# Spreading the RMS reciprocals over the partitions: one fp32 diagonal in four 128-column products, or two fp32r diagonals in two 512-column products

## The chip, the cores and the metric

One core of one Trainium2 chip runs the whole kernel. The metric is the device time of one execution in microseconds (us). Engines are named as the profile names them: PE is TensorE (PEld its weight load), DVE is VectorE, ACT is ScalarE, POOL is GpSimd, SP is the queue that issues most DMAs.

## What is computed

One layer of a hybrid decoder trunk over 1024 tokens of width 1024, in float32. Two RMS norms, one before the input projection and one behind the output projection, are what the change is about:

```python
def rms_norm(x, g):
    xf = x.astype(jnp.float32)
    y = xf * lax.rsqrt(jnp.mean(xf * xf, axis=-1, keepdims=True) + NORM_EPS)
    return (y * g.astype(jnp.float32)).astype(x.dtype)

h = rms_norm(x, g_pre[i])
proj = h @ w_in[i]            # six slices: S5, LRU and merge-gate inputs
...                           # S5 branch -> z_s, RG-LRU branch -> z_l
merged = jax.nn.sigmoid(gate_s) * z_s + jax.nn.sigmoid(gate_l) * z_l
x = x + rms_norm(merged @ w_out[i], g_post[i])
x = x + (p[i] @ w_ple[i]) * jax.nn.sigmoid(x @ w_ple_gate[i])
```

## The kernel before

Everything is kept transposed: channels lie on the 128 partitions, tokens on the free axis, in two halves of 512 tokens (`HT`). A float32 product is made of three products of fp32r parts (`three`, lines L316 and L318): each operand is split into a high part, which ACT writes by a copy into an fp32r tile, and a low part, which DVE (or a DMA with an accumulate, lines L225 and L226) forms as value minus high part. Weights come in blocks of 128x128, four to a "quad" `wq`; the class `Weights` loads them into four raw buffers, splits them (L222 on ACT, L234 on DVE) and keeps six quads in a ring, so that they are made some quads ahead of their use.

PE, DVE, ACT and POOL are in a manual schedule: each runs its instructions in the order in which the code writes them. Work that is to run beside the products of PE is written as generators; `tick()` takes one step of each between quads.

The statistics of a norm are made by `tok_rstd`, a generator in three steps. First PE sums the squares over the partitions, so that the sums of 128 tokens stand in one column of a PSUM tile `pst` (L388). Then DVE and ACT compute, on 8 columns (4 for a half), the variance, the square root (L393, ACT), its reciprocal and one Newton step (L394 to L398), and DVE multiplies the identity by each column, which gives one 128x128 diagonal for 128 tokens (L401). In the third step a matrix of ones times each diagonal (L406) puts the reciprocal of every token on all partitions, in a PSUM tile `psb` for each half.

It is called three times.

- **pre**, at the start of the kernel, for all 1024 tokens. At that time PE computes the eight rows `ps_ple` of `p @ w_ple` (m = 0 to 7, 12 products each), in PSUM tiles of 1024 columns of which there are three (`pw2`); row m = 7 uses the tile of row m = 4. ACT copies each row to SBUF (`evict`, L743). The second step of `tok_rstd` stands in the code behind the products of m = 5 and ahead of the evictions of m = 4 and m = 5; the third stands in the middle of the products of m = 7. Behind it `h_hi` (L727 on DVE, L728 on ACT) and `h_lo` (L733) normalise x and split it, for the first products of the input projection (`ps_u`).
- **post1**, for the second half of the tokens, beside the last products of the output projection (`oV`). Its results feed a chain of steps on DVE and ACT (`post_half`), one for each of the eight channel blocks: mix times `psb` (L1562), times the gain plus the residual (L1563), the high part on ACT (L1364), the low part on DVE (L1371). The first products of the gate (`ps_pg`) follow it.
- **post0**, for the first half, beside the products of the gate for the second half. On ACT a sigmoid of a finished gate row (L1589) stands right behind its square root, with the load of the table for it; on DVE the product and the sum with that row (L1590, L1591) stand ahead of the chain of post0.

Of the kernel before, what the change touches and what calls it, by code (L numbers as in the profile page):

```python
# [9 lines left out]
F32 = mybir.dt.float32  # L10
F32R = mybir.dt.float32r
I32 = mybir.dt.int32
AF = mybir.ActivationFunctionType
ALU = mybir.AluOpType
# [3 lines left out]
P = 128  # L18
NT = 1024
HT = 512  # L20
ND = 8
# [114 lines left out]
class Weights:  # L136
# [99 lines left out]
    def next(self):  # L236
        self.make(self.pos)
        self.lows(self.pos)
        t = self.done[self.pos]
        n = QUADS[self.pos][3]  # L240
        self.pos += 1
        return [(t[:, 0, b, :], t[:, 1, b, :]) for b in range(n)]
# [10 lines left out]
def tile_hybrid_trunk(  # L253
# [11 lines left out]
    V, S, G, T = nc.vector, nc.scalar, nc.gpsimd, nc.tensor  # L265
# [10 lines left out]
    def page(i, name, dt=F32R):  # L276
        return page_pool[i].tile([P, 2 * NT], dt, tag=f"pg{i}", name=name)
# [10 lines left out]
    def cst(shape, name, value=None, dt=F32):  # L288
        t = const.tile(shape, dt, name=name)
        if value is not None:  # L290
            V.memset(t, value)
        return t

    ones = cst([P, P], "ones", 1.0)
    ident = cst([P, P], "ident")
    make_identity(nc, ident)
    halfpi = cst([P, 1], "halfpi", math.pi / 2)
    cp_t = cst([P, sum(n for _, n in CPAR)], "cp_t")
    sp8 = cst([P, NL], "sp8")
    nsp8 = cst([P, NL], "nsp8")  # L300
    cp = {}
    o = 0
    for nm, n in CPAR:
# [19 lines left out]
    def bank(name):  # L323
        return pp.tile([P, HT], F32, tag="pp", name=name)
# [58 lines left out]
    def tok_rstd(v, ssqs, n, name, res, diag):  # L383
        nch = n // P
        ps = px.tile([P, HT], F32, tag="px", name=f"pst_{name}")
        for c in range(nch):
            for j, ssq in enumerate(ssqs):
                T.matmul(ps[:, c:c + 1], ssq[:, c * P:(c + 1) * P], ones[:, 0:1], start=j == 0, stop=j == len(ssqs) - 1)  # L388
        yield
        v = v.rearrange("p (i n) -> p i n", i=4)  # L390
        var, r, t, sd = (v[:, i, :nch] for i in range(4))
        V.tensor_scalar(var, ps[:, :nch], 1.0 / (ND * P), EPS, ALU.mult, ALU.add)
        S.activation(sd, var, AF.Sqrt)  # L393
        V.reciprocal(r, sd)  # L394
        V.tensor_tensor(t, r, r, ALU.mult)
        V.tensor_tensor(t, t, var, ALU.mult)
        V.tensor_scalar(t, t, -0.5, 1.5, ALU.mult, ALU.add)
        V.tensor_tensor(r, r, t, ALU.mult)  # L398
        diag = diag.rearrange("p (c t) -> p c t", c=nch)
        for c in range(nch):  # L400
            V.tensor_scalar(diag[:, c, :], ident, r[:, c:c + 1], None, ALU.mult)  # L401
        yield
        for h in range(n // HT):
            pb = px.tile([P, HT], F32, tag="px", name=f"psb_{name}_{h}")
            for c in range(4):
                T.matmul(pb[:, c * P:(c + 1) * P], ones, diag[:, 4 * h + c, :], start=True, stop=True)  # L406
            res.append(pb)
        yield

# [40 lines left out]
    def quarter(t):  # L450
        return t.rearrange("p (k n) -> p k n", n=HT)
# [7 lines left out]
    pro = pctx.enter_context(tc.tile_pool(name="pro", bufs=1))  # L459
    x_half = [pool.tile([P, 4, NT], F32, name=f"xt{i}") for i, pool in enumerate((pro, prob))]  # L460

    def xt(k, s=slice(0, NT)):
        return x_half[k // 4][:, k % 4, s]

    def two_rows(i, name, dt=F32):
        return page(i, name, dt).rearrange("p (k n) -> p k n", k=2)

    sdp = two_rows(9, "sdp")
    ssq = sdp[:, 0]
# [4 lines left out]
    NPAR = sum(n for _, n in SPAR)  # L474
    NPT = NPAR - 2048
    pt = scratch[:, :NPT]
    braw = page(7, "braw", F32)

    ET = mybir.EngineType
    ctx.enter_context(tc.manual_schedule(engines={ET.PE, ET.DVE, ET.Activation, ET.Pool}))  # L480
# [221 lines left out]
    def square(k):  # L702
        sq = sqs[k % 2][:, k // 2 % 2] if k else ssq
        if k in (1, 3):
            (V if k == 1 else G).tensor_tensor(sq, xt(k), xt(k), ALU.mult)
        else:
            S.activation(sq, xt(k), AF.Square)
        if k:
            adds.append(sq)
# [4 lines left out]

    rb = []
    ssqs = [ssq]
    stats = tok_rstd(pro.tile([P, 4 * ND], F32, name="rs_pre"), ssqs, NT, "pre", rb, sdp[:, 1])
    hq = {}

    def hplain(k, h):  # L720
        hi, lo = hq[f"B{1 + k // 4}{1 + h}"]
        return hi[:, k % 4, :], lo[:, k % 4, :]

    def h_hi(k):
        for h in range(2):
            xs = xt(k, HALF[h])
            V.scalar_tensor_tensor(xs, xs, gpre[:, k:k + 1], rb[h], ALU.mult, ALU.mult)  # L727
            S.activation(hplain(k, h)[0], xs, AF.Copy)  # L728
# [12 lines left out]
    def evict(m):  # L741
        sb = ple_sb[m // 2][:, m % 2]
        S.activation(sb, rows_ps[m], AF.Copy)  # L743
        nc.sync.dma_start(ple_d[m], sb)
# [34 lines left out]
    h_lo(0)  # L779
    evict(7)  # L780
    h_hi(1)
    nc.sync.dma_start(braw[:, :1024], spar[:, NPT:NPT + 1024])
    S.activation(d_skip, pt[:16, NPT - 32:], AF.Copy)

# [448 lines left out]
    def ysr(j):  # L1233
        return ysf[j // 2][:, j % 2]
# [28 lines left out]
    for j in range(NS):  # L1263
        t, y = et[:, j % 2], ysr(j)
# [22 lines left out]
    PG = (9, 18, 11, 2, 3, 16, 17, 4, 5, 12, 13, 10, 14, 15, 0, 1, 6, 7, 8)  # L1287
# [19 lines left out]
    for p_ in range(4):  # L1307
# [9 lines left out]
        z, w_, v = (bank(f"b{n}{p_}") for n in "ZWV")  # L1317
# [28 lines left out]
    def quads8(idx, name):  # L1346
        t = [[quarter(page(idx[2 * s + q], f"{name}{s}{q}")) for q in range(2)] for s in range(2)]
        return lambda s, k: t[s][k // 4][:, k % 4, :]
# [3 lines left out]
    def mgrow(d):  # L1352
        return mgt[d // 2][:, d % 2]
# [9 lines left out]
    def lagged(lo, src, hi):  # L1363
        S.activation(hi, src, AF.Copy)  # L1364
        late.append((lo, src, hi))
        flush(1)

    def flush(n=0):
        while len(late) > n:
            lo, src, hi = late.pop(0)  # L1370
            V.tensor_tensor(lo, src, hi.bitcast(F32), ALU.subtract)  # L1371
# [41 lines left out]
    for n, d in enumerate(F_ROWS):  # L1413
        if n:
            sgs_load()
        for h, ps in enumerate(brows(ysr_, f"F{d}", NS)):
            r = mgrow(d)[:, HALF[h]]
# [15 lines left out]
    def x1(k, h):  # L1433
        return x1p[k // 2][:, k % 2, HALF[h]]
# [20 lines left out]
    def last_op():  # L1455
# [12 lines left out]
    sq, ssq = ([t[:, HALF[i]] for i in range(2)] for t in (  # L1468
        h2.tile([P, NT], F32, tag=f"g{j}", name=n) for j, n in enumerate(("sq", "ssq"))))
    counts, pending = [0, 0], [[], []]  # L1470

    def mixt(row, h):
        if mix[h][row // 4] is None:
            mix[h][row // 4] = quarter(page(PG[((0, 2), (18, 11))[h][row // 4]], f"mix{h}{row // 4}", F32))
        return mix[h][row // 4][:, row % 4, :]
# [11 lines left out]
    def add_square(h):  # L1487
        for t in pending[h]:
            V.tensor_tensor(ssq[h], ssq[h], t, ALU.add)
        pending[h].clear()  # L1490
# [53 lines left out]
    def post_half(h):  # L1544
        out_ = []
        while squares[h]:
            square(h, squares[h].pop(0))
            yield
        add_square(h)
        st = tok_rstd(dg[:, 2, 32 * h:32 * h + 32], [ssq[h]], HT, f"post{h}", out_, dg[:, h, :])  # L1550
        if h == 0:
            yield
        next(st)
        next(st)
        yield
        for _ in st:
            pass
        rb = out_[0]
        x1hl[h] = hl = quads8(mpg[h], f"x1hl{h}")
        for k in range(ND):  # L1560
            mk = mixt(k, h)
            V.tensor_tensor(mk, mk, rb, ALU.mult)  # L1562
            V.scalar_tensor_tensor(x1(k, h), mk, gpost[:, k:k + 1], x1(k, h), ALU.mult, ALU.add)  # L1563
            lagged(hl(1, k), x1(k, h), hl(0, k))
            if k == ND - 1:
                flush()
            yield
# [44 lines left out]
                    V.tensor_tensor(sb[:, q], sb[:, q], x1(m, h)[:, q], ALU.add)  # L1612
                nc.sync.dma_start(out[m * P:(m + 1) * P, h * HT + cs.start:h * HT + cs.stop], sb[:, cs])

    dg = quarter(page(PG[1], "diags", F32))
    bg.append(post_half(1))
    for name, row in (("T4", 1), ("T4", 3), ("T4", 5), ("T4", 7), ("B21", 4), ("B21", 6)):
        c, ps = mixt(row, 0), bank(f"oV{row}")
# [3 lines left out]
    plp, sbp = (quarter(page(PG[i], n, F32)) for i, n in ((9, "plp"), (10, "sbp")))  # L1622
    drain()
    bg.append(post_half(0))
    gate_half(1, x1hl[1])
    drain()
# [68 lines left out]
```

## Time and profile before

| | |
|---|---|
| median of 3 runs | 932.66 us (932.24 to 932.68) |
| the profiled execution | 932.37 us, of which the span of its instructions is 930.6 us |
| PE busy | 923.1 us of the span (99%), 4228 matmuls |
| DVE busy | 625.0 us (67%) |
| ACT busy | 469.6 us (50%) |
| POOL busy | 150.3 us (16%) |
| granted TensorE clock, mean | 0.999 |

A timeline row reads: start and duration in us, engine, line, operation, output and inputs, form, count of merged instructions, and in square brackets the idle time of the engine before it with what ended it. Successive matmuls overlap in the records, so the distance between starts is what a matmul costs in a stream, not its duration. The same holds for successive ACT instructions, whose starts lie a little closer than their durations.

### The profile page before, as it was taken

What the parts mean: (1) busy time and instruction counts of PE and PEld (TensorE: products, weight loads), DVE (VectorE), ACT (ScalarE), POOL (GpSimd) and SP (SyncE); (2) the same over time, 40 slices, a digit from 0 to 9 for tenths busy, and PEclk for the clock granted to TensorE, in tenths of its full rate; (3) what the DMA queues carried; (4) which work ended last, traced back from release to release, by engine and by line L of the source; (5) the groups of instructions that cost most, each with busy time, mean ns of one, the idle gap of its engine ahead of it and who ended that gap; (6) DMA issues with size and microseconds to landing.
All of it is one profiled execution on the core that took longest, in us unless ns stands there. A gap on an engine that the chain in (4) does not pass through costs nothing.

```text
span 930.6 us, 11716 instructions
## 1 busy us (share of the span) xinstructions
PE 923.1 (99%) x4228; PEld 759.7 (82%) x4228; DVE 625.0 (67%) x977; ACT 469.6 (50%) x714; POOL 150.3 (16%) x159
## 2 busy tenths in 40 slices
PE   9999999999999999999999999999999999999997
PEld 7888888888888888888888888888888887887876
DVE  6985566666664446776666667687862798886863
ACT  6643233444443257666666668444434355558531
POOL 1318012212220000000000000022322126422100
PEclk9999999999999999999999999999999999999999
DMA  9745456554623211111111117811479965499951
GB/s 356 277 126 158 126 141 168 173 166 138 178 90 107 74 29 52 51 51 45 52 51 51 52 44 208 296 41 57 141 261 238 271 164 203 122 244 231 301 181 52
DMA packets 70442, 134.21 MB, mean 144 GB/s; under 512 B 18416, under 2 KB 32880, under 8 KB 70384
## 3 DMA queue, kind: packets, MB, share of 16 engines
q1 hardware_dynamic: 64768, 122.72, 41.5%
q0 software_dynamic: 5472, 10.49, 6.5%
q8 instruction: 33, 0.54, 0.2%
q10 hardware_dynamic: 144, 0.26, 0.1%
q14 instruction: 25, 0.20, 0.1%
HBM read 95.30 MB, written 27.53 MB: 132 GB/s over the span
## 4 chain that ended last, share of the span: by engine, by line
PE 96%; DVE 2%; issue 0%; DMA 0%; ACT 0%
PE ps_L L318 16%; PE ps_L L316 8%; PE ps_rg L318 8%; PE ps_rx L318 8%; PE ps_pg L318 6%; PE ps_rx L316 4%; PE ps_rg L316 4%; PE ps_F L318 3%; PE ps_u L318 3%; PE bZ L318 3%; PE ps_pg L316 3%; PE pg L318 2%; PE bW L318 2%; PE bX L318 2%; PE ps_ple L318 2%; PE ps_ea L318 2%
## 5 line engine op out<-in xcount | busy, mean ns | idle before, releaser
L318 PE MATMUL ps_L<-hB,wq 128*128 128x512 f32 x640 | 197.4, 390 | 0.0
L318 PEld LDWEIGHTS ps_L<-hB,wq 128*128 128x128 f32 x640 | 120.2, 188 | 24.5
L316 PE MATMUL ps_L<-hB,wq 128*128 128x512 f32 x320 | 127.0, 397 | 0.0
L222 ACT ACTIVATE wq<-wraw 128x512 fp32r<-128x512 f32 (+1 forms) x188 | 112.5, 614 | 24.3 <-issue 9.4
L234 DVE TENSOR_TENSOR wq<-wraw,wq 128x512 fp32r<-128x512 f32 (+1 forms) x152 | 104.0, 700 | 3.2 <-ACT wq L222 3.2
L318 PE MATMUL ps_rg<-hB,wq 128*128 128x512 f32 x320 | 98.7, 390 | 0.0
L318 PE MATMUL ps_rx<-hB,wq 128*128 128x512 f32 x320 | 98.7, 390 | 0.0
L318 PE MATMUL ps_pg<-x1hl,wq 128*128 128x512 f32 x240 | 75.2, 394 | 0.5 <-DVE x1hl L1371 0.5
L316 PEld LDWEIGHTS ps_L<-hB,wq 128*128 128x128 f32 x320 | 60.1, 188 | 13.4 <-issue 1.7
L318 PEld LDWEIGHTS ps_rg<-hB,wq 128*128 128x128 f32 x320 | 60.1, 188 | 12.9
L318 PEld LDWEIGHTS ps_rx<-hB,wq 128*128 128x128 f32 x320 | 60.1, 188 | 12.9
L1075 DVE SCALAR_TENSOR_TENSOR c<-ps_rx,cp_t,c 128x1023 f32<-128x1023 f32 (+2 forms) x30 | 38.5, 1282 | 47.6 <-ACT c L1073 46.9
L194 POOL TENSOR_TENSOR wS<-wraw 128x512 f32<-128x512 f32 x8 | 11.9, 1486 | 356.8 <-DMA wraw<-w_blocks 349.4
L316 PE MATMUL ps_rx<-hB,wq 128*128 128x512 f32 x160 | 62.5, 391 | 0.0
L316 PE MATMUL ps_rg<-hB,wq 128*128 128x512 f32 x160 | 62.5, 391 | 0.0
L318 PEld LDWEIGHTS ps_pg<-x1hl,wq 128*128 128x128 f32 x240 | 44.7, 188 | 11.8 <-DVE x1hl L1371 1.8
L1012 ACT ACTIVATE sg<-ps_L 128x1024 f32<-128x1024 f32 x20 | 20.5, 1026 | 59.6 <-issue 52.5
L226 POOL DMA_DIRECT2D wq<-wraw x36 | 31.8, 883 | 100.7 <-ACT wq L225 68.7
L316 PE MATMUL ps_pg<-x1hl,wq 128*128 128x512 f32 x120 | 47.1, 393 | 0.0
L318 PE MATMUL ps_u<-hB,wq 128*128 128x512 f32 x128 | 39.7, 392 | 0.4 <-DVE hB L733 0.4
L318 PE MATMUL ps_F<-ys,wq 128*128 128x512 f32 x128 | 39.4, 389 | 0.0
L1083 ACT ACT_TABLE_LOAD x9 | 11.5, 1283 | 51.2 <-DVE yr L1112 51.2
(360 smaller groups left out, 1930.4 us busy)
## 6 DMA issues: line engine op xcount, KB each, us to landing
wraw<-w_blocks SPq DMA_DIRECT2D x95, 512.0 KB
wq<-wraw POOLq DMA_DIRECT2D x36, 256.0 KB, 5.5
xt<-x_t SPq DMA_DIRECT2D x8, 512.0 KB
ple_d<-ple_sb SPq DMA_DIRECT2D x8, 512.0 KB
wn<-sbt SPq DMA_DIRECT2D x8, 512.0 KB
sgl_d<-sg SPq DMA_DIRECT2D x8, 512.0 KB
wn<-pt_d SPq DMA_DIRECT2D x16, 256.0 KB
sgs_d<-sg SPq DMA_DIRECT2D x8, 512.0 KB
```

The costliest lines, as they stand in the source:

```text
L194: G.tensor_tensor(s[name], s[a], s[b], op)
L222: nc.scalar.activation(hi, src, AF.Copy)
L226: nc.gpsimd.dma_start(lo.bitcast(F32), src, accum_op=ALU.add)
L234: self.nc.vector.tensor_tensor(lo, src, hi.bitcast(F32), ALU.subtract)
L316: T.matmul(ps, wh, xh, start=start, stop=False, skip_group_check=more)
L318: T.matmul(ps, a, b, start=False, stop=stop and a is (wh if xl_last else wl), skip_group_check=more)
L1012: S.activation(t, ps, AF.Sigmoid)
L1075: V.scalar_tensor_tensor(c[:, d:], ps[:, :NT - d], w_[3 - d], c[:, d:], ALU.mult, ALU.add)
L1083: S.activation(sq, ps, AF.Sigmoid)
```

## The change

The reciprocal r is split into a high part, rounded to fp32r (a cast on DVE), and the remainder (a subtraction on DVE). Each part gets a diagonal of its own: the high one by DVE, as before, the low one by ACT, as a copy of the identity with a scale taken from the column (8 such instructions in pre, 4 in each post). The spread then takes two products of fp32r for each half of 512 tokens, the ones matrix times the high diagonals and, accumulated, times the low ones, in place of four fp32 products of 128 columns. The ones matrix is cast to fp32r once at the start. The diagonals of pre move from the tile `sdp` to a tile `spread` on page 7, and the later tile of that page, `braw`, is taken after them.

The computing lines move by a few in the new file: L393 becomes L397, L401 becomes L408, the new ACT copies are L409, L406 becomes L414, L743 becomes L751, L728 becomes L736.

```diff
     ones = cst([P, P], "ones", 1.0)
     ident = cst([P, P], "ident")
+    ones_r = cst([P, P], "ones_r", dt=F32R)
+    V.tensor_copy(ones_r, ones)
+    rhl = cst([P, ND], "rhl", dt=F32R)
...
+    rs_post = cst([P, 40], "rs_post")
...
-        v = v.rearrange("p (i n) -> p i n", i=4)
+        v = v.rearrange("p (i n) -> p i n", i=5)
...
-        diag = diag.rearrange("p (c t) -> p c t", c=nch)
+        dh, dl = (t_.rearrange("p (c t) -> p c t", c=nch) for t_ in diag)
+        rh, rl = rhl[:, :nch], v[:, 4, :nch]
+        V.tensor_copy(rh, r)
+        V.tensor_tensor(rl, r, rh.bitcast(F32), ALU.subtract)
         for c in range(nch):
-            V.tensor_scalar(diag[:, c, :], ident, r[:, c:c + 1], None, ALU.mult)
+            V.tensor_scalar(dh[:, c, :], ident, r[:, c:c + 1], None, ALU.mult)
+            S.activation(dl[:, c, :], ident, AF.Copy, scale=rl[:, c:c + 1])
         yield
         for h in range(n // HT):
             pb = px.tile([P, HT], F32, tag="px", name=f"psb_{name}_{h}")
-            for c in range(4):
-                T.matmul(pb[:, c * P:(c + 1) * P], ones, diag[:, 4 * h + c, :], start=True, stop=True)
+            for d, e in zip(diag, (True, False)):
+                T.matmul(pb, ones_r, d[:, h * HT:(h + 1) * HT], start=e, stop=not e)
...
-    braw = page(7, "braw", F32)
+    spread = page(7, "spread").rearrange("p (i n) -> p i n", i=2)
...
-    stats = tok_rstd(pro.tile([P, 4 * ND], F32, name="rs_pre"), ssqs, NT, "pre", rb, sdp[:, 1])
+    stats = tok_rstd(pro.tile([P, 5 * ND], F32, name="rs_pre"), ssqs, NT, "pre", rb, (spread[:, 0], spread[:, 1]))
...
+    braw = page(7, "braw", F32)
     nc.sync.dma_start(braw[:, :1024], spar[:, NPT:NPT + 1024])
...
-        st = tok_rstd(dg[:, 2, 32 * h:32 * h + 32], [ssq[h]], HT, f"post{h}", out_, dg[:, h, :])
+        st = tok_rstd(rs_post[:, 20 * h:20 * h + 20], [ssq[h]], HT, f"post{h}", out_, (dg[:, 2 * h, :], dg[:, 2 * h + 1, :]))
...
-    dg = quarter(page(PG[1], "diags", F32))
+    dg = quarter(page(PG[1], "diags"))
```

On ACT, at pre, the row of the square root and what follows it, before. `ps_ple_264` and `ps_ple_282` are the PSUM rows m = 4 and m = 5, `wq_321` to `wq_342` the quads for the first `ps_u`:

```order
L393 ACTIVATE rs_pre<-rs_pre 128x8
L743 ACTIVATE ple_sb_117<-ps_ple_264 128x1024
L222 ACTIVATE wq_321<-wraw_194 128x512
L743 ACTIVATE ple_sb_117<-ps_ple_282 128x1024
L222 ACTIVATE wq_339<-wraw_194 128x512
L222 ACTIVATE wq_342<-wraw_218 128x512
L728 ACTIVATE hB_368<-xt_107 128x512
```

The same place after, where row m = 4 is `ps_ple_268`:

```order
L397 ACTIVATE rs_pre<-rs_pre 128x8
L409 ACTIVATE spread<-ident,rs_pre 128x128 x8
L751 ACTIVATE ple_sb_121<-ps_ple_268 128x1024
L222 ACTIVATE wq_335<-wraw_198 128x512
L751 ACTIVATE ple_sb_121<-ps_ple_286 128x1024
L222 ACTIVATE wq_353<-wraw_198 128x512
L222 ACTIVATE wq_356<-wraw_222 128x512
L736 ACTIVATE hB_378<-xt_111 128x512
```

Eight copies have come between the square root and the eviction of row m = 4.

On PE, at the same place, after, with the waits that stand in the instructions: the first product of row m = 7 (`ps_ple_359`), and the spread in the middle of that row:

```order
L320 MATMUL ps_ple_359<-p_hi,wq_281 128x512 [waits Activation_49]
L322 MATMUL ps_ple_359<-p_lo,wq_281 128x512
L322 MATMUL ps_ple_359<-p_hi,wq_281 128x512
L320 MATMUL ps_ple_359<-p_hi,wq_281 128x512
L322 MATMUL ps_ple_359<-p_lo,wq_281 128x512
L322 MATMUL ps_ple_359<-p_hi,wq_281 128x512
L414 MATMUL psb_pre_366<-spread,ones_r 128x512 [waits DVE_49]
L414 MATMUL psb_pre_366<-spread,ones_r 128x512
L414 MATMUL psb_pre_369<-spread,ones_r 128x512 [waits DVE_49,PE_49]
L414 MATMUL psb_pre_369<-spread,ones_r 128x512
L320 MATMUL ps_ple_359<-p_hi,wq_281 128x512
```

The row's first product waits for ACT as it did before; only the four L414 rows are new, in place of eight L406.

On ACT, at post0, before; the sigmoid is that of a finished gate row:

```order
L225 ACTIVATE wq_6706<-wraw_6522 128x512
L393 ACT_TABLE_LOAD
L393 ACTIVATE diags<-diags 128x4
L1589 ACT_TABLE_LOAD
L1589 ACTIVATE sbp<-ps_pg_1_6688 128x512
L222 ACTIVATE wq_6746<-wraw_6579 128x512
```

And after:

```order
L225 ACTIVATE wq_6721<-wraw_6537 128x512
L397 ACT_TABLE_LOAD
L397 ACTIVATE rs_post<-rs_post 128x4
L409 ACTIVATE diags<-ident,rs_post 128x128 x4
L1598 ACT_TABLE_LOAD
L1598 ACTIVATE sbp<-ps_pg_1_6703 128x512
L222 ACTIVATE wq_6767<-wraw_6594 128x512
```

Four copies stand ahead of the table load and the sigmoid.

## The prediction

> **What bounds the kernel now.** The page first: the span, the busy times, the shares of the chain that ended last.
>
> ```profile
> span 930.6 us, 11716 instructions
> ...
> PE 923.1 (99%) x4228; PEld 759.7 (82%) x4228; DVE 625.0 (67%) x977; ACT 469.6 (50%) x714; POOL 150.3 (16%) x159
> ...
> PE 96%; DVE 2%; issue 0%; DMA 0%; ACT 0%
> ```
>
> PE is the bound, with 2% of the chain on DVE. So a shorter product helps where PE is never kept waiting, and any new wait of PE adds to the time. The 2% must be looked for around the three calls of `tok_rstd`. The timeline there, at pre (columns: start, duration):
>
> ```profile
> 4.88 0.43 DVE L523 CAST p_hi<-pf 128x512 fp32r<-128x512 f32 x1 [3.87 <-DMA pf<-p_t]
> ...
> 7.30 0.63 PE L316 MATMUL ps_ple<-p_hi,wq 128*128 128x512 f32 x1
> 7.73 0.63 PE L318 MATMUL ps_ple<-p_hi,wq 128*128 128x512 f32 x1
> ...
> 10.05 0.40 PE L318 MATMUL ps_ple<-p_hi,wq 128*128 128x512 f32 x1
> 10.28 0.39 PE L318 MATMUL ps_ple<-p_lo,wq 128*128 128x512 f32 x1
> ...
> 26.55 0.21 ACT L393 ACTIVATE rs_pre<-rs_pre 128x8 f32<-128x8 f32 x1 [3.53 <-DVE rs_pre L392]
> 26.67 1.01 ACT L743 ACTIVATE ple_sb<-ps_ple 128x1024 f32<-128x1024 f32 x1
> ...
> 27.57 0.62 ACT L222 ACTIVATE wq<-wraw 128x512 fp32r<-128x512 f32 x1
> 27.64 0.17 DVE L398 TENSOR_TENSOR rs_pre<-rs_pre 128x8 f32<-128x8 f32 x1
> ...
> 27.84 1.66 DVE L401 TENSOR_SCALAR sdp<-ident,rs_pre 128x128 f32<-128x128 f32 x8
> ...
> 29.00 1.15 ACT L222 ACTIVATE wq<-wraw 128x512 fp32r<-128x512 f32 x2
> 29.03 0.39 PE L316 MATMUL ps_ple<-p_hi,wq 128*128 128x512 f32 x1
> ...
> 29.41 1.89 DVE L234 TENSOR_TENSOR wq<-wraw,wq 128x512 fp32r<-128x512 f32 x3
> ...
> 30.39 1.95 PE L406 MATMUL psb_pre<-sdp,ones 128*128 128x128 f32 x16
> 31.49 1.64 DVE L727 SCALAR_TENSOR_TENSOR xt<-xt,cp_t,psb_pre 128x512 f32<-128x512 f32 x2 [0.18 <-PE psb_pre L406]
> ...
> 32.10 0.48 PE L316 MATMUL ps_ple<-p_hi,wq 128*128 128x512 f32 x1
> ...
> 33.16 0.64 ACT L728 ACTIVATE hB<-xt 128x512 fp32r<-128x512 f32 x1 [0.20 <-DVE xt L727]
> ...
> 38.64 0.73 PE L318 MATMUL ps_u<-hB,wq 128*128 128x512 f32 x2 [0.39 <-DVE hB L733]
> ```
>
> Three things are to be seen. The row at 29.03 is the first product of m = 7; until then PE never waits. From 31.49 DVE and ACT run back to back (L727, L728, L733), and PE catches up with them: at 38.64 it stands waiting for them. And on ACT the eviction of m = 4 (26.67) follows right behind the square root.
>
> **The price of one low-part copy on ACT** (128x128, fp32r out, scale from a column). No row shows it; the nearest, grouped by shape (mean ns before the bar's idle time):
>
> ```profile
> L222 ACT ACTIVATE wq<-wraw 128x512 fp32r<-128x512 f32 x178 | 109.5, 625 | 24.3 <-issue 9.4 <-DMA wraw<-w_blocks 5.1 <-PE bX L318 4.3
> ...
> L1094 ACT ACTIVATE i<-pg,cp_t 128x512 f32<-128x512 f32 x20 | 13.8, 688 | 0.0
> ...
> L1589 ACT ACTIVATE sbp<-ps_pg 128x512 f32<-128x512 f32 x15 | 8.8, 591 | 24.7 <-PE ps_pg L318 24.6
> ...
> L222 ACT ACTIVATE wq<-wraw 128x256 fp32r<-128x256 f32 x10 | 4.1, 410 | 0.0
> ```
>
> 512 and 256 columns differ by 0.215, so 128 columns are 0.410 - 0.108 = 0.30 us. A column operand (the bias of L1094 against L1589, both sigmoids) adds 0.10. That makes 0.40 us; starts lie closer than that by 0.11 (1.01 long at 26.67, the next at 27.57). I take 0.295 us per copy. Bounds: 0.10 (L393's 0.21 less the overlap) and 0.50 (the 256-column row with the column operand and no overlap).
>
> **The change, part by part.**
>
> The cast of the ones on DVE lies in the 3.87 us in which DVE waits for its first data (row at 4.88): nothing. The move of `braw` is costed at nothing too: its DMA goes out behind pre, and its reader stands in the S5 parameters, behind the `ps_u` products.
>
> *PE's products.* At pre 16 records of L406 took from 30.39 to 32.10, 1.71 us; four of 512 columns take 4 x 0.23 (10.05 to 10.28) = 0.92, saving 0.79 if PE has its inputs.
>
> *Pre.* On DVE the cast and the subtraction go between L398 and the diagonals, 0.20 each (27.64 to 27.84), so the remainder is there at 28.24. ACT has meanwhile finished its square root, and its next instructions are now the copies: it idles until 28.24, works 8 x 0.295 = 2.36, and starts the eviction of m = 4 at 30.60 instead of 26.67. That is 3.93 late; it ends at 31.61. Row m = 7 needs that PSUM tile, so PE stands from 29.03 to 31.6. Behind the eviction on ACT are one more and three L222; the end of the last moves from 30.15 (29.00 + 1.15) to 34.08. DVE's third L234 waits for that, which lets L727 begin at 34.08 + 0.03 + 0.60 = 34.71 (before 31.49) and its second at 35.35, ending at 36.1. The second L728, at 33.16 before, comes at 36.12: 2.96 late, less than 3.93 because before, the second L727 waited for PE's spread and L234 had work in hand. From there to 38.64 the chain is as before, and PE waits at its end, so the loss is **+2.96**. PE's 0.79 is not seen: the spread would end at about 34.1, ahead of L727. With the bounds of the copy: 1.4 to 4.6.
>
> *Post1.*
>
> ```profile
> 821.01 0.16 DVE L398 TENSOR_TENSOR diags<-diags 128x4 f32<-128x4 f32 x1
> ...
> 822.44 1.05 PE L406 MATMUL psb_post<-diags,ones 128*128 128x128 f32 x8
> ...
> 823.25 0.48 PE L316 MATMUL oV<-mT,wq 128*128 128x512 f32 x1
> ...
> 823.53 0.69 DVE L1562 TENSOR_TENSOR mix<-mix,psb_post 128x512 f32<-128x512 f32 x1 [0.85 <-PE psb_post L406]
> ...
> 825.04 0.63 ACT L1364 ACTIVATE x1hl<-x 128x512 fp32r<-128x512 f32 x1 [3.82 <-DVE x L1563]
> ...
> 841.95 0.73 PE L318 MATMUL ps_pg<-x1hl,wq 128*128 128x512 f32 x2 [0.47 <-DVE x1hl L1371]
> ```
>
> PE's products here took 0.81 (822.44 to 823.25), and two at 0.23 take 0.46: 0.35 less, at post0 as well, so that PE has 1.5 us less to do in all three places. The remainder is ready at 821.6; four copies end at 821.6 + 3 x 0.295 + 0.40 = 822.88. PE's high product can start at 822.55, the low one at 822.92, and with 0.39 of its own duration L1562 starts at 823.35, 0.18 earlier than before. DVE's two small steps fit into its 0.85 of idle time. The chain of DVE from 823.53 ends in PE's wait at 841.95, so this counts: **-0.18** (bounds -0.3 and +0.6). The one quad whose split stands behind the copies on ACT comes 2.7 us late, but ACT is idle for 3.82 before 825.04, so no more than that one is.
>
> *Post0.*
>
> ```profile
> 858.64 1.28 ACT L1589 ACT_TABLE_LOAD   x1
> ...
> 859.47 0.16 DVE L398 TENSOR_TENSOR diags<-diags 128x4 f32<-128x4 f32 x1
> ...
> 859.94 0.60 ACT L1589 ACTIVATE sbp<-ps_pg 128x512 f32<-128x512 f32 x1
> ...
> 860.57 0.69 DVE L1590 TENSOR_TENSOR sbp<-sbp,plp 128x512 f32<-128x512 f32 x1
> ...
> 865.05 0.61 ACT L1364 ACTIVATE x1hl<-x 128x512 fp32r<-128x512 f32 x1
> 865.57 0.57 ACT L1589 ACTIVATE sbp<-ps_pg 128x512 f32<-128x512 f32 x1
> ...
> 866.17 0.69 DVE L1590 TENSOR_TENSOR sbp<-sbp,plp 128x512 f32<-128x512 f32 x1 [0.76 <-ACT sbp L1589]
> ...
> 884.63 1.48 DVE L1371 TENSOR_TENSOR x1hl<-x,x1hl 128x512 fp32r<-128x512 f32 x2
> ...
> 885.37 0.30 PEld L318 LDWEIGHTS ps_pg<-x1hl,wq 128*128 128x128 f32 x2 [0.43 <-DVE x1hl L1371]
> ```
>
> Before, the table load ran while DVE made the diagonals. Now the copies stand ahead of it: remainder at 860.05, copies from 860.07 to 861.35, table 1.28, sigmoid at 862.66 instead of 859.94. L1590 waits for it on DVE (860.57 was just behind the sigmoid's end at 860.54), and behind L1590 stand L1591 and the whole chain from L1562 on. All of it goes 2.72 late. Can it be recovered before 885? DVE's idle 0.76 at 866.17 looks like room, but that sigmoid (865.57) stands on ACT behind L1364, which waits for DVE: the loop is closed. At 885.37 PE already waits for the low parts made at 884.63. So **+2.72** (1.9 to 3.5), and PE's 0.35 is swallowed there.
>
> Sum, from the profiled execution's 932.37: + 2.96 - 0.18 + 2.72 = 937.87. That execution lies 0.29 under the median of 932.66. I say **937.9**. The bounds together give 935.4 to 941.1.
>
> **Rivals.**
>
> *The clock.* PE's first products step by 0.43 (7.30, 7.73), later ones by 0.23 (10.05, 10.28). If a wait of some 2.6 us throws it back to the slow step for as long as the rows show it (2.8 us from 7.30 to 10.05, at least) it loses 1.3 us or more at each place; with 2 us each 939.9 to 942. Against it: the waits are short, and that at post0 comes in pieces. No run so far shows a wait of this length behind the start. The Trainium skill (TensorE: Matmul & The Clock Gate, Part 1) states that the clock falls to half after one idle window of about 3.4 us and needs as long a busy one to return; by that rule waits of 2.6 us are mostly spared, and the sum stays as it is. The slow step at the start agrees with its half rate.
>
> *Only one place counts*: with post0 made good before 885 the sum ends at 932.37 + 2.96 - 0.18 = 935.2, with pre made good before 38.64 at 934.9.
>
> *Not slower.* PE has 99% of the span, and ACT only 50%; were the copies and all behind them covered, only PE's 1.5 us would be left: 930.9. The point that decides is slack of 3.0 us on DVE ahead of 38.64 and 2.7 ahead of 885.37; the rows show PE waiting at both, so none. A copy below 0.10 us does not reach it either, since ACT's wait for the remainder alone is 1.57.
>
> *Later still*: the quads made late on ACT at post0 land late by the accumulating DMA, and PE waits for them before 885 and again after: 940 or more.
>
> **Chances.** Forecast 0.62, one place only 0.12, clock 0.12, not slower 0.08, later still 0.06. The range 934.8 to 941.2 holds the forecast with its bounds, the single places and the nearer half of the clock. A measurement of this kernel can tell 0.2%, 1.9 us, from no change; 930.9 lies at that edge, so not slower splits in faster 0.03 and same 0.05, and all else is slower, 0.92.
>
> **What would show it.** Right: in the changed profile ACT idle about 1.5 us behind the square root of pre, L409 stepping by about 0.3, PE waiting some 2.6 us for ACT's eviction ahead of m = 7, the sigmoid of post0 2.7 us further behind the square root, and PE waiting about 3 us in all for DVE's low parts around 885 plus the shift. Wrong: PE products of 0.23 step all through 26 to 40 with no wait, or low parts at post0 that are in time.

## The result and the profile after

The change made the kernel slower: 939.16 us, median of four runs (938.29 to 942.58), against 932.67 (932.24 to 932.71). The ratio is 1.0079, with an interval of 1.0066 to 1.0091. A second measurement of the same kernel, on another occasion, gave 938.48 (937.83 to 939.47, five runs) against 932.32: ratio 1.0064 (1.0052 to 1.0077). The forecast was 937.9, in a range of 934.8 to 941.2.

The profiled execution took 938.29, 0.4 more than the sum of the prediction. Its page, the span, the busy times and the shares of the chain that ended last:

```profile
span 936.5 us, 11690 instructions
...
PE 923.4 (99%) x4204; PEld 757.7 (81%) x4204; DVE 625.8 (67%) x984; ACT 474.3 (51%) x730; POOL 150.8 (16%) x159
...
PE 88%; DVE 5%; DMA 4%; ACT 1%; issue 1%; POOL 0%; SPq 0%; DVEq 0%; ACTq 0%; POOLq 0%
```

PE's busy time hardly moved (923.1 before), and ACT has only 4.7 us more to do. The span grew by 5.9 us all the same, and PE's share of the chain fell from 96% to 88%: the time went into waits. The view of PE's waits (total in us, times, longest) has these four rows, of which the kernel before had at most half a microsecond each:

```profile
PE ps_ple L320 <- ACT ple_sb L751: 2.4, 1, 2.4
PE ps_pg L322 <- DVE x1hl L1380: 1.8, 2, 1.4
PE ps_pg L322 <- DMA wq<-wraw: 0.9, 1, 0.9
PE ps_u L320 <- ACT hB L736: 0.7, 1, 0.7
```

The timeline, in three pieces, at pre, post1 and post0 (start, duration; in brackets the idle time before and what ended it). L397 is the square root, L406 the subtraction, L409 the low copies, L414 the spread products, L751 the eviction, L735 and L736 the former L727 and L728, L1380 the former L1371, L1571 the former L1562, L1598 and L1599 the former L1589 and L1590.

```profile
26.61 0.21 ACT L397 ACTIVATE rs_pre<-rs_pre 128x8 f32<-128x8 f32 x1 [3.64 <-DVE rs_pre L396]
...
28.31 2.44 ACT L409 ACTIVATE spread<-ident,rs_pre 128x128 fp32r<-128x128 f32 x8 [1.48 <-DVE rs_pre L406]
...
30.66 1.00 ACT L751 ACTIVATE ple_sb<-ps_ple 128x1024 f32<-128x1024 f32 x1
...
31.71 0.50 PE L320 MATMUL ps_ple<-p_hi,wq 128*128 128x512 f32 x1 [2.45 <-ACT ple_sb L751]
...
33.21 1.09 PE L414 MATMUL psb_pre<-spread,ones_r 128*128 128x512 f32 x4
...
34.85 1.40 DVE L735 SCALAR_TENSOR_TENSOR xt<-xt,cp_t,psb_pre 128x512 f32<-128x512 f32 x2
...
41.75 0.73 PE L322 MATMUL ps_u<-hB,wq 128*128 128x512 f32 x2 [0.25 <-DVE hB L741]
...
826.60 0.69 DVE L1571 TENSOR_TENSOR mix<-mix,psb_post 128x512 f32<-128x512 f32 x1 [0.53 <-PE psb_post L414]
...
861.47 0.20 ACT L397 ACTIVATE rs_post<-rs_post 128x4 f32<-128x4 f32 x1 [0.31 <-DVE rs_post L396]
...
863.12 1.28 ACT L409 ACTIVATE diags<-ident,rs_post 128x128 fp32r<-128x128 f32 x4 [1.45 <-DVE rs_post L406]
864.42 1.28 ACT L1598 ACT_TABLE_LOAD   x1
865.72 0.60 ACT L1598 ACTIVATE sbp<-ps_pg 128x512 f32<-128x512 f32 x1
...
866.35 0.69 DVE L1599 TENSOR_TENSOR sbp<-sbp,plp 128x512 f32<-128x512 f32 x1 [2.47 <-ACT sbp L1598]
...
882.78 0.50 PE L322 MATMUL ps_pg<-x1hl,wq 128*128 128x512 f32 x1 [0.85 <-DMA wq<-wraw]
...
890.35 1.47 DVE L1380 TENSOR_TENSOR x1hl<-x,x1hl 128x512 fp32r<-128x512 f32 x2
...
891.09 0.72 PE L322 MATMUL ps_pg<-x1hl,wq 128*128 128x512 f32 x2 [1.40 <-DVE x1hl L1380]
```

What is to be seen: the copies stand on ACT exactly where the order put them. At pre the eviction that PE needs starts at 30.66 instead of 26.67; at post0 the sigmoid that DVE needs starts at 865.72 instead of 859.94 (3.05 of that was brought along from the stages before). Each time a row with a bracket shows who stood waiting: PE for 2.45, DVE for 2.47. PE had no more work in any of it. (Of the 1.8 for low parts 1.40 is at post0; the other 0.4 is at post1, where the kernel before waited 0.47.)

### The profile page after: what moved, and what is told of

It reads as the page before. It is cut to its first block, busy times and chain, and to the rows that moved or that the text cites. A ratio compares the mean times of both kernels' runs of the same rounds, so it can differ in the third digit from the quotient of the medians.

```text
span 936.5 us, 11690 instructions
## 1 busy us (share of the span) xinstructions
PE 923.4 (99%) x4204; PEld 757.7 (81%) x4204; DVE 625.8 (67%) x984; ACT 474.3 (51%) x730; POOL 150.8 (16%) x159
## 4 chain that ended last, share of the span: by engine, by line
PE 88%; DVE 5%; DMA 4%; ACT 1%; issue 1%; POOL 0%; SPq 0%; DVEq 0%; ACTq 0%; POOLq 0%
PE ps_L L322 16%; PE ps_L L320 8%; PE ps_rg L322 8%; PE ps_rx L322 8%; PE ps_pg L322 4%; PE ps_rx L320 4%; PE ps_rg L320 4%; PE ps_u L322 3%; PE bZ L322 3%; PE ps_pg L320 2%; PE pg L322 2%; PE bW L322 2%; PE bX L322 2%; DMA msr<-ms_d 2%; PE ps_ea L322 2%; PE ps_eb L322 2%
## 5 line engine op out<-in xcount | busy, mean ns | idle before, releaser
L222 ACT ACTIVATE wq<-wraw 128x512 fp32r<-128x512 f32 (+1 forms) x188 | 112.4, 613 | 24.2 <-issue 9.4
```

The source lines that it names most:

```text
L222: nc.scalar.activation(hi, src, AF.Copy)
```

## The experiments

In all of them *shift* means: the start of one product of PE in the kernel at hand minus that of the same product in the kernel before. The change has a shift of 3.11 at 41.75, 5.72 at 891.09 and 5.94 at the last product. A trace is of one execution, so a shift can differ from what the median of the runs says.

**One place at a time.** `pre_only` gives `tok_rstd` its old code back for the two posts, `post_only` for pre:

```diff
+        old = not isinstance(diag, tuple)
...
+        if old:
+            for c in range(nch):
+                V.tensor_scalar(diag[:, c, :], ident, r[:, c:c + 1], None, ALU.mult)
+            yield
...
+                for c in range(4):
+                    T.matmul(pb[:, c * P:(c + 1) * P], ones, diag[:, 4 * h + c, :], start=True, stop=True)
...
+            return
         dh, dl = (t_.rearrange("p (c t) -> p c t", c=nch) for t_ in diag)
```

> The new spread at pre alone, both posts as before. Theory (ACT's copies delay the eviction of m = 4, and with it PE and the chain into ps_u): the profile of the changed kernel shows PE 3.1 us late at the end of that stage, so 932.7 + 3.1 = 935.8 (935.2 to 936.4). Rival, all of the loss at post0: 932.7. Rival, the clock: the runs of the changed kernel spread from 938.3 to 942.6 with mean granted clocks of 1.000 down to 0.995; if PE's wait of 2.4 us ahead of m = 7 sets that off, the runs of this kernel spread as far, with the same fall of the clock in the slow ones; if the waits at post0 do, they agree within 0.5 us.

> The new spread at both posts, pre as before. Theory: the sigmoid of post0 behind the copies and the table load makes the DVE chain 2.7 us late, and PE waits at its end: 932.7 + 2.7 = 935.4 (934.9 to 935.9). Rival, all of the loss at pre: 932.5. The clock: if PE's wait at pre sets it off, these runs agree within 0.5 us at one mean clock.

Against 932.42 (931.94 to 933.29), `pre_only` took 936.04 (934.78 to 936.88), ratio 1.0037 (1.0025 to 1.005), and `post_only` 934.58 (934.11 to 936.23), ratio 1.0025 (1.0016 to 1.0035). Both places cost, and the two excesses, 3.6 and 2.2, add up to 5.8, near the whole change's 6.5 and 6.2. So *only one place counts* falls. The five runs of `pre_only` lie 2.1 us apart, and the longest, 936.88, has a mean clock of 1.000: I had expected 0.5 at most unless the clock fell, so something else than the clock also spreads the runs, and it was not found. The waits of PE in `pre_only` are those of pre alone; the low parts near 885 are again nearly in time, as they were before:

```profile
PE ps_ple L320 <- ACT ple_sb L764: 2.5, 1, 2.5
...
PE ps_u L320 <- ACT hB L749: 0.7, 1, 0.7
...
PE ps_pg L322 <- DVE x1hl L1393: 0.4, 1, 0.4
```

`post_only` came out 0.8 under its expectation in the median, and outside the bounds given. Its trace gives post0 its price all the same: the shift is -0.55 just ahead of post0, where mostly a slow drift had brought it, and 2.10 behind PE's wait at 887.47, so 2.65. Its profiled execution, 935.81, was one of the longer ones, and shows what made it longer. The timeline of PE there, and then the windows around it (length, busy time of PE, PEld, DVE, ACT and POOL, and at the end of a row PE's granted clock, the DMA share and GB/s):

```profile
885.45 0.40 PE L320 MATMUL ps_pg<-x1hl,wq 128*128 128x512 f32 x1
...
887.47 1.08 PE L322 MATMUL ps_pg<-x1hl,wq 128*128 128x512 f32 x2 [1.62 <-DVE x1hl L1392]
888.36 0.63 PE L320 MATMUL ps_pg<-x1hl,wq 128*128 128x512 f32 x1
```

```profile
885.00:887.60 2.60, 0.97 (x4) 0.50 (x5) 2.47 (x5) 1.17 (x3) 0.00 (x0) 1.00 0.55 186
887.60:891.10 3.50, 3.50 (x9) 2.73 (x10) 3.46 (x6) 2.63 (x6) 0.00 (x0) 0.51 0.32 101
891.10:895.00 3.90, 3.90 (x19) 3.17 (x18) 2.13 (x4) 0.41 (x1) 0.00 (x0) 1.00 0.88 265
```

Behind the wait the clock is 0.51 for 3.5 us, and products take 0.63 instead of 0.40. The shift grows from 2.1 to 3.5 there. That is the clock of the prediction's first rival, after a wait of only 1.62.

**Only the copies on ACT.** `act_dummy` is the kernel before, with the copies added on ACT at the places of the change, into a spare tile that nobody reads; `braw` is taken late, as in the change. The products are the old ones.

```diff
             V.tensor_scalar(diag[:, c, :], ident, r[:, c:c + 1], None, ALU.mult)
+            S.activation(spare[:, c * P:(c + 1) * P], ident, AF.Copy, scale=r[:, c:c + 1])
```

> The kernel before, with its fp32 diagonals and products, and only the copies on ACT added at their places (8 at pre, 4 at each post, of the identity scaled by r into a spare tile that nothing reads; no cast, no subtraction). Theory: what costs is the copies' place in ACT's order. They start 0.4 us earlier than in the change, since r is ready 0.4 earlier: pre + 2.6, post0 + 2.3, together 937.6 (936.8 to 938.4). Rival, the form of the products on PE or the fp32r operands cost the time: 932.7.

It took 938.63 (937.46 to 938.98), ratio 1.0064 (1.005 to 1.0077): the copies alone cost as much as the whole change, 1 us above what I expected and just above its upper end. Its timeline at pre, and one row of PE from much later:

```profile
27.82 2.45 ACT L402 ACTIVATE spare<-ident,rs_pre 128x128 f32<-128x128 f32 x8 [1.08 <-DVE rs_pre L398]
...
30.18 1.00 ACT L744 ACTIVATE ple_sb<-ps_ple 128x1024 f32<-128x1024 f32 x1
...
775.57 0.51 PE L318 MATMUL oY<-mT,wq 128*128 128x512 f32 x1 [0.78 <-DVE wq L234]
```

The eviction is late again (26.67 to 30.18), and the shift behind it is 2.63, at the end 5.42. In this execution (937.78) the two places cost what I had forecast: 2.63 at pre (2.6 forecast), and 2.25 at post0, where the shift goes from 3.17 to 5.42 (2.3 forecast). Another 0.52 came between them, where PE waited for the low part of a quad (775.57); that the copies cause this wait is not shown. The new products, the cast and the subtraction are not needed for the loss.

**Everything but the copies.** `no_low` makes one fp32r diagonal and one product of 512 columns per half. It leaves the remainder of the rstd out.

```diff
-        rh, rl = rhl[:, :nch], v[:, 4, :nch]
-        V.tensor_copy(rh, r)
-        V.tensor_tensor(rl, r, rh.bitcast(F32), ALU.subtract)
...
-            S.activation(dl[:, c, :], ident, AF.Copy, scale=rl[:, c:c + 1])
...
-            for d, e in zip(diag, (True, False)):
-                T.matmul(pb, ones_r, d[:, h * HT:(h + 1) * HT], start=e, stop=not e)
+            T.matmul(pb, ones_r, diag[0][:, h * HT:(h + 1) * HT], start=True, stop=True)
```

> The change without the low part: one fp32r diagonal by DVE and one 512-column product for each half, no copies on ACT, no cast, no subtraction (this leaves out the remainder of r, so the norm is only as exact as fp32r). It shows what the shorter products are worth at most. Theory: at pre the second L735 no longer waits for PE, - 0.4; at post1 the DVE chain starts 0.6 earlier; post0 stands behind the sigmoid's chain, 0. Together 931.6 (931.2 to 932.2). Rival, PE's saved product time counts in full: 1.25 + 2 x 0.58 = 2.4 less, 930.3.

It took 931.49 (931.05 to 932.24), ratio 0.9989 (0.998 to 0.9998), 0.9 under the kernel before and inside the expected range. One row of its timeline says where PE's saving stops:

```profile
31.32 1.40 DVE L729 SCALAR_TENSOR_TENSOR xt<-xt,cp_t,psb_pre 128x512 f32<-128x512 f32 x2
```

DVE begins 0.17 earlier than before (31.49) and its two steps take 1.40 instead of 1.64. The shift is -0.42 behind pre; behind the spread of post0 it reaches -1.4, and PE then waits it down to -0.34 for quads and low parts around 880. A cheaper product in those places pays only up to the next wait.

**The copies elsewhere on ACT.** `post0_late` runs post0's low copies behind the sigmoid, on the same engine; `both_late` does so too, and at pre puts them behind the eviction of m = 4 and the three L222. The diff is that of `both_late`.

```diff
+        def lows():
+            for c in range(nch):
+                S.activation(dl[:, c, :], ident, AF.Copy, scale=rl[:, c:c + 1])
+        later.append(lows)
+        if name not in ("pre", "post0"):
+            later.pop()()
...
                 S.activation(sb[:, cs], ps, AF.Sigmoid)
+                while later:
+                    later.pop()()
...
-    A, E, Q = square, evict, weights
+    A, E, Q, L = square, evict, weights, lambda _: later.pop()()
...
-            5: ((E, 4), (Q, 4)),
-            6: ((E, 5), (Q, 5), (Q, 6)),
+            5: ((E, 4), (Q, 4), (Q, 5), (Q, 6), (L, 0)),
+            6: ((E, 5),),
```

> The changed kernel with one move: the four low-part copies of post0 stand behind the sigmoid on ACT, ahead of nothing but two weight splits; everything else as in the change. Theory: of post0's loss only the 0.4 us of the cast and the subtraction ahead of L1599 on DVE are left, so the loss goes from 5.7 to some 3.4: 936.1 (935.5 to 936.7), and the shift of PE in the trace does not grow by more than 0.6 us between 860 and 890. Rival, the copies as such slow ACT and DVE wherever they stand: 938.5 to 939.

> The move at post0, and at pre the eight copies behind the eviction of m = 4 and the three weight splits L222, ahead of the eviction of m = 5. Theory: the eviction of m = 4 is then in time, so PE does not wait ahead of m = 7; the copies end at about 31.5, the spread waits for them some 1.1 us, the second L735 ends about 0.3 to 0.5 later than in the kernel before. Pre + 0.4, post0 + 0.4: 933.3 (932.8 to 934.0). Rival, the loss at pre is in the cast, the subtraction and the products: 935.5 to 936.

`post0_late`, against 932.24 (931.97 to 933.0): 936.12 (935.31 to 936.7), ratio 1.0038 (1.0024 to 1.0052), as expected; in its trace the shift grows by 0.36 over post0 (3.75 to 4.11). `both_late`: 932.52 (931.81 to 933.88), ratio 1.0003 (0.9994 to 1.0012), no change that can be told from none, and 0.8 under the 933.3 expected, just below its range. Timeline of `post0_late` at post0, and of `both_late` at pre:

```profile
863.68 0.60 ACT L1607 ACTIVATE sbp<-ps_pg 128x512 f32<-128x512 f32 x1
864.18 1.26 ACT L414 ACTIVATE diags<-ident,rs_post 128x128 fp32r<-128x128 f32 x4
864.48 0.68 DVE L1610 TENSOR_TENSOR sbp<-sbp,plp 128x512 f32<-128x512 f32 x1
```

```profile
26.61 1.01 ACT L760 ACTIVATE ple_sb<-ps_ple 128x1024 f32<-128x1024 f32 x1
27.52 1.66 ACT L222 ACTIVATE wq<-wraw 128x512 fp32r<-128x512 f32 x3
29.07 2.44 ACT L414 ACTIVATE spread<-ident,rs_pre 128x128 fp32r<-128x128 f32 x8
...
31.57 0.50 PE L423 MATMUL psb_pre<-spread,ones_r 128*128 128x512 f32 x1 [0.38 <-ACT spread L414]
```

The same twelve copies, of the same length, cost nothing that the times can show once the eviction and the sigmoid stand ahead of them. PE now waits for the copies themselves, 0.38, where I had expected 1.1: the high products, and the first half's low one, could go ahead. The shift behind pre is -0.27. This is the most direct evidence for the cause: nothing but the order of the work (that of the copies on ACT and of two weight splits with them) differs between 932.5 and 939.2 (or 938.5). What the two moved splits alone do in the kernel before was not run, so how much of the -0.27 is theirs stays open.

**The clock behind the waits.** `post_fill` is `post_only` with eight products whose result nobody reads, of 512 columns, placed where PE waits for the low parts. `both_fill` is the change with the same eight, and ten more ahead of m = 7. The diff shows the eight.

```diff
+            if not h and k == 6 and not filled:
+                filled.append(1)
+                fill = px.tile([P, HT], F32, tag="px", name="fill")
+                for _ in range(8):
+                    T.matmul(fill, hl(0, 0)[:, :P], hl(0, 0), start=True, stop=True)
```

> The kernel with the change at the posts alone (934.6 us; its profiled run shows PE waiting 1.6 us at the sixth block and then 3.4 us at half clock, and its ten runs have mean clocks from 1.000 to 0.995), with eight idle products of 512 columns put into PE's order just ahead of that block, 1.8 us of work in place of the wait. Theory (the wait sets the clock back in some runs): mean clock 0.998 or more in every run, none above 935.0, median 934.3 to 934.6. Rival, the slow runs have another cause: again some at 0.997 or less and above 935.5. If the idle products are not hidden by the wait, 936.3.

> The changed kernel once more, unaltered, for more runs with their mean clocks: two profiles (post_only at post0, post0_late at pre) have shown the clock at half for 3.4 us behind PE's wait. Theory: most runs at 938.3 to 939.5, and those with a mean clock of 0.997 or less above 939.5, up to 942.6. Rival: the spread does not go with the clock.

> The changed kernel with idle products in PE's order in both waits: ten of 512 columns (2.3 us) ahead of row m = 7 at pre, eight (1.8 us) ahead of the sixth block at post0. Theory: the chains on ACT and DVE set the time as before, so the runs stay at 938.2 to 938.8, but with no wait long enough to set the clock back none is above 939.2 and no mean clock is below 0.998. Rival: the spread to 942.6 has another cause and stays; or the idle products cost their own time, 942.

`post_fill`: 934.42 (933.9 to 935.1, ten runs), ratio 1.0024 (1.0014 to 1.0033), every mean clock at least 0.999; the highest run is 0.1 over the bound of my expectation. `post_only` had reached 936.23, with clocks down to 0.995. The medians, 934.42 and 934.58, show no cost of the idle products. Timeline in `post_fill`:

```profile
886.57 1.98 PE L1598 MATMUL fill<-x1hl 128*128 128x512 f32 x8
887.23 1.48 DVE L1392 TENSOR_TENSOR x1hl<-x,x1hl 128x512 fp32r<-128x512 f32 x2
888.38 0.39 PE L320 MATMUL ps_pg<-x1hl,wq 128*128 128x512 f32 x1
```

The product behind them takes 0.39, the full rate. In this execution the filling was too long, though: PE had come late to it (behind a wait of 1.03 for a quad, at 880.05), the low part was there at about 887.97 (half of the row at 887.23), and PE's first product that reads it starts at 888.61, 0.64 later.

What ties the slow stretch to the wait is its place: in three traces (`post_only`, `after_again` and `post0_late`, below) the half clock begins within about 1 us behind a wait of PE. That filling the wait keeps the stretch away is not shown by these runs: two of the ten of `post_only` have a mean clock of 0.997 or less and none of the ten of `post_fill`, which chance can give too; and two of the 20 runs of the kernel before that were taken beside `post_fill` are at 0.997, though its trace has no such wait.

`after_again`, the change unaltered, gave the 938.48 of the first section; its profiled execution (939.47, mean clock 0.997) shows a third wait, and the clock behind it. Timeline of PE and one window:

```profile
877.03 0.39 PE L322 MATMUL ps_pg<-x1hl,wq 128*128 128x512 f32 x1
879.36 0.50 PE L322 MATMUL ps_pg<-x1hl,wq 128*128 128x512 f32 x1 [1.94 <-DMA wq<-wraw]
...
880.83 1.05 PE L322 MATMUL ps_pg<-x1hl,wq 128*128 128x512 f32 x2
```

```profile
880.30:883.80 3.50, 3.50 (x10) 2.68 (x9) 3.43 (x7) 1.15 (x2) 0.00 (x0) 0.51 0.84 242
```

The shift goes from 4.17 over 6.25 (the wait for a quad) to 7.98 (the half clock, 1.73), and ends at 7.11. The two runs with a mean clock of 0.997 are the longest of the five (939.47 and 939.09), but 939.5, which I had expected them to pass, neither reaches.

`both_fill` took 938.08 (937.37 to 938.94), ratio 1.0056 (1.0043 to 1.007). It does not tell more: the interval overlaps that of the change, and four of its five runs lie below the 938.2 to 938.8 that I had expected. The profiled execution, 938.94 with a mean clock of 0.997, had its half clock at the start of the kernel (0.51 from 7.3 to 10.8), where nothing was changed, so my expectation that no mean clock would lie below 0.998 failed. A low mean clock does not say by itself, then, where the clock fell. The timeline shows PE's wait of 2.45 ahead of m = 7 filled at almost no cost:

```profile
29.21 2.43 PE L772 MATMUL fill<-p_hi,wq 128*128 128x512 f32 x10
31.83 0.50 PE L321 MATMUL ps_ple<-p_hi,wq 128*128 128x512 f32 x1 [0.19 <-ACT ple_sb L752]
```

PE, busy but for 0.19, starts m = 7 at 31.83, nearly as in the change (31.71): the time there is set by ACT. At post0 the eight products ran too long here too: the low part was there at about 891.73 (half of a DVE row of 1.47 that starts at 890.99), and PE read it at 892.58.

## Why the prediction was right, point by point

*Pre, +2.96.* Measured as the shift of the product that waits for the second half of `h`: 41.75 - 38.64 = 3.11. The copy was estimated at 0.295 from two sizes of other activations; eight starts span 28.31 to 30.66, 0.294 each. The idle time behind the square root came out at 1.48 (about 1.5 expected), PE's wait for the eviction at 2.45 (2.6). The spread took PE from 33.21 to the start of the next product at 34.14, 0.93 (0.92 forecast), and DVE's L735 began at 34.85, later than that, as forecast (34.71). `both_late` shows that the order on ACT made the term, `pre_only` that it reaches the end (3.04 of shift at 888.41 and 2.39 at the last product in its trace, 3.6 between the medians).

*Post1, -0.18.* L1571 starts 3.07 after L1562 did, with 3.12 of shift brought along: -0.05. The sign held; the size is too small to be worth a cause.

*Post0, +2.72.* The sigmoid starts 5.78 later than before; the statistic itself was 3.05 late there, which leaves 2.73. At 890.35 the low parts are 5.72 late: nothing was made good in between. That fits the loop that the prediction named, in which DVE's L1599 waits for a sigmoid that stands on ACT behind a step waiting for DVE: its next round still idles 0.76, as before. One sign came out lower than named: PE waits 1.40 for DVE's low parts there and not about 3, with another 0.85 for a quad just before (882.78); together they carry the shift from 3.05 to 5.72. The excess of `post_only` is 2.2 and not 2.5 (-0.18 + 2.72), within its interval.

*The sum.* 932.37 + 5.50 = 937.87 against 938.29 profiled: 0.15 from pre, 0.13 from post1, the rest behind 891, where PE waits a little more. That the parts add up so closely is in part luck: the 3.11 from pre had drifted to 2.64 by 769, and a wait of PE for a quad there happened to bring it back to 3.11 by 775. The two medians, 939.16 and 938.48, lie 1.3 and 0.6 above the forecast. What can lengthen single executions is next.

*The clock (chance 0.12).* It was put as an alternative, and it is an addition that comes and goes. The profiled execution of the change has waits of 2.45 and 1.40 and no slow stretch; `post_only` has one behind 1.62, `after_again` behind 1.94, and `post0_late` behind the wait at pre. There the windows of `post0_late` read:

```profile
29.00:31.80 2.80, 0.34 (x2) 0.27 (x2) 0.65 (x4) 2.80 (x8) 0.00 (x0) 1.00 0.00 0
31.80:35.30 3.50, 3.50 (x10) 2.71 (x10) 2.19 (x4) 2.14 (x4) 0.00 (x0) 0.51 0.74 300
```

The stretch costs 1.4 to 1.7 where PE is the bound. Behind the wait at pre it costs 0.44: from the first product of m = 7 to the product that waits at 41.75 in the change, the shift grows by 0.87 in `post0_late` (2.50 to 3.37), and by 0.42 or 0.43 in the four traces that have this wait and no slow stretch behind it (the change, `after_again`, `pre_only`, `act_dummy`). That it is less there fits that ACT and DVE set the time. The prediction leaned on the Trainium skill (TensorE: Matmul & The Clock Gate, Part 1) for the sentence that waits of 2.6 us are mostly spared. The half rate and the length of about 3.4 us that the Trainium skill gives there agree with the windows (0.51 over 3.5 us); its condition, one idle window of about 3.4 us, does not, for no idle stretch of that length stands in these places, and the clock fell behind waits of 1.62 and 1.94 in some executions. The measurement decides: a wait of this length is a risk, not a safe one. The rows that the prediction quoted from the start of the kernel gave the right price, and its "with 2 us each" was too dear.

*Later still (0.06).* Something like it is seen in small: PE waits for a quad for 0.85 at 882.78, which the later wait at 891.09 swallows, and 1.94 in `after_again`, which it does not wholly. That the late copies cause it is argued, not shown: `no_low` has a wait of 0.9 for a quad's transfer too, though there PE came early.

*Not slower (0.08).* It falls by every row above; `both_late` is what it would have looked like, and it asked for another order, not for slack.

*What stays open.* The 942.58 of the first four runs (mean clock 0.995) has no trace. Two slow stretches and a late quad would make it, but nobody saw them in that execution. Between 304 and 769 the shift falls from 3.35 to 2.64 in the change, and by about as much in `pre_only`, `post_only` and `both_late`, but not in `act_dummy`; in the change it returns at a wait for a quad. No run was spent on that.

## What to carry to other kernels

An engine that is idle half of the time still runs in order: what new work on it costs is read from the instruction that it is put in front of and from who waits for that, not from the engine's share of the span. Put such work behind the evictions and activations that the bounding engine needs; here that alone was worth 6 us, and left no cost that the times can show. Where a short wait of PE can't be removed, filler products can take its place; here they cost nothing that the medians show and held PE by 0.64 us in the execution where PE came to them late, and whether they keep the clock up is open. Look first whether PE is what sets the time there.

## What the hardware showed that I had not expected

PE's granted clock can fall to 0.51 for some 3.4 us behind a wait as short as 1.62 us, in some executions and not in others with waits as long (the change's own trace has 2.45 and 1.40 and no fall). Its price depends on the place: 1.4 us in `post_only` and 1.73 in `after_again`, 0.44 behind the wait at pre in `post0_late`.
